# A hybrid attention and mLSTM layer: the FFN in chunks of three and six token blocks, with seven half-size float16 products for the gate and up rows of the six

## The chip, the cores and the metric

The kernel runs on one core of a Trainium2 chip. The core has a matrix engine (PE), whose weight loads are listed as PEld, a vector engine (DVE), an activation engine (ACT), a general engine (POOL), and a queue engine (SP) that issues most DMAs. The metric is device time in microseconds, lower is better; a kernel's time is the median of several runs. Traces come from one profiled execution each.

## The reference

One layer over 9 blocks of 128 tokens (block 0 context, blocks 1 to 8 latent), D = 1024, D_FF = 2816, all in float32. Cut to what matters:

```python
def trunk_layer(x, mods, ...):
    sh1, sc1, g1, sh2, sc2, g2 = mods
    h = rmsnorm(x, norm1_w) * (1 + sc1) + sh1
    aq, ak, av, mq, mk, mv, mo, mg = jnp.split(h @ w_in, SPLIT_POINTS, axis=-1)
    ...
    attn_o = attention(aq, keys, vals)              # 8 query heads, 2 kv heads, 64 wide
    hm, st_f, st_b = mlstm_bidir(...)               # 4 heads, 128 wide, both directions
    ...
    mix = jnp.concatenate([attn_o, hm], axis=-1) @ w_out
    x = x + g1 * mix
    h2 = rmsnorm(x, norm2_w) * (1 + sc2) + sh2
    x = x + g2 * swiglu(h2, w_gu, w_down)

def swiglu(h, w_gu, w_down):
    g, u = jnp.split(h @ w_gu, 2, axis=-1)
    return (jax.nn.silu(g) * u) @ w_down
```

Latent tokens read 128 context keys and all 1024 latent keys. A final norm gives the outputs.

## The kernel before

Float32 accuracy comes from pairs: a value is split into a high part (a cast) and a low part (value minus high), and a product is three matmuls, high with high, high with low, low with high. The input projection has float16 pairs with a common power-of-two scale per weight group; the output projection and the FFN have fp32r pairs without a scale. `load_piece` brings a piece of weights from HBM into `raw` (2 buffers), casts it on ACT into `whi` and subtracts on POOL, or on DVE for each third piece, into `wlo` (5 buffers each). `sub` (L137) is the one line of all such subtractions.

Stages: modulation and normed inputs; query, key, value projections; four mLSTM heads, each head's projection woven with the scan of the head before and with attention of blocks 0 to 2; the mLSTM half of the output projection for all blocks (`prefill`); then the FFN in three chunks of three blocks (`CB` = 3). In a chunk, 22 row tiles f of 128 come in groups of 4 or 5. For each f, `gate_up` runs 24 matmuls for gate and 24 for up over 384 tokens (`products`, L1315 to L1317), applies tanh-form SiLU (L1333 to L1335) and splits the result into `hl`. After a group, `down` multiplies it with `w_down` for both halves n of the output (L1115 to L1117) and adds the gated sum to x1 (`add_gated`, L1104 and L1105).

Beside the first chunk the attention of blocks 3 to 5 is woven in, beside the second that of blocks 6 to 8; behind each comes `attn_out`, the attention half of the output projection, and `norm2` of the next chunk beside the last down group. In attention (`attention`), a head's scores S (L1035, one PSUM tile of three banks) go to DVE for the maximum (L1037), ACT for the exponential (L1038) and the scaled cast (L1041), DVE for the low part (L1042), two DMA transposes, and later 18 value products for a pair of heads (L1059, L1060).

What sets the order: the program is written as generators, `weave` advances a side generator at a rate beside a main one, `hot` raises a priority, and a scheduler orders each engine's instructions by priority and modelled readiness. Every engine then runs its list strictly in order. Buffers are tagged tiles in pools; a new tile waits for the last user of the tile that it replaces.

## Time and profile before

| what | us |
|---|---|
| median of 3 runs (1592.95 to 1603.68) | 1601.16 |
| the profiled execution | 1606.1 |
| its span in the trace | 1604.4 |
| first gate product | 642.1 |
| granted PE clock, mean | 0.973 of full |

The trace is read by stage: the FFN chunks start at 642.1, 963.4 and 1315.3 us. HBM traffic is 183.8 MB read and 13.3 MB written; the largest transfers are 132 gate and up pieces and 72 down pieces, most of 512 KB. Busy time of an engine says little by itself, since matmul records overlap; the distance between starts is a matmul's price in a dense run. Engines other than PE can be idle without cost where PE never waits for them.

### The profile page before, as it was taken

Reading aid. Unit: us, or ns where it says so; the run is one execution under the profiler, and the core shown is the slowest. Engines: PE = TensorE matmul, PEld = TensorE weight load, DVE = VectorE, ACT = ScalarE, POOL = GpSimd, SP = SyncE. Lnnn points to the kernel's source line nnn. Section 1 sums busy time; section 2 is a strip of 40 time slices with the busy share of each in tenths; the row PEclk is TensorE's granted clock in tenths of the full one; section 3 lists DMA queues with packets and bytes.
Section 4 is the critical chain, followed back from the end, with each engine's and each line's share of the span. In section 5 each row is a group of like instructions: output and inputs, shape, how many; then the busy total and the mean of one; then the engine's idle time right before and its main releaser. Section 6 shows DMA issues by size and latency. Waiting matters only on the chain. (4 is left out here: it accounts for less than half of the span.)

```text
span 1604.4 us, 23368 instructions
## 1 busy us (share of the span) xinstructions
PE 1502.1 (94%) x8539; PEld 1252.0 (78%) x8539; DVE 929.7 (58%) x1856; ACT 767.1 (48%) x1409; POOL 658.9 (41%) x526
## 2 busy tenths in 40 slices
PE   6888989899988779999999999999999999999996
PEld 3544557676766567989999989899898989899995
DVE  4778545745747575567443556777764474332445
ACT  4844455856655354535432444555562453333322
POOL 0243532333343443544444444443444445544443
PEclk9899999899999899999999999999999999999998
DMA  9474323442555736867653456887674455544442
GB/s 359 155 198 153 95 53 42 102 77 51 83 138 159 250 106 145 210 173 184 164 153 127 141 151 211 197 179 178 153 177 129 128 151 165 153 128 146 144 128 70
DMA packets 387880, 236.91 MB, mean 148 GB/s; under 512 B 170198, under 2 KB 346790, under 8 KB 387766
## 3 DMA queue, kind: packets, MB, share of 16 engines
q1 hardware_dynamic: 385110, 231.84, 53.7%
q10 hardware_dynamic: 2656, 3.58, 1.0%
q8 instruction: 67, 1.10, 0.3%
q14 instruction: 47, 0.39, 0.1%
HBM read 183.79 MB, written 13.26 MB: 123 GB/s over the span
## 5 line engine op out<-in xcount | busy, mean ns | idle before, releaser
L137 POOL TENSOR_TENSOR wlo<-raw,whi 128x1024 fp32r<-128x1024 f32 (+1 forms) x144 | 349.6, 2431 | 418.3 <-ACT whi L154 392.1
L154 ACT CAST whi<-raw 128x1024 fp32r<-128x1024 f32 (+1 forms) x216 | 221.6, 1026 | 386.3 <-DMA raw<-in_w_gu_dram 136.5
L1316 PE MATMUL mm<-aTl,whi 128*128 128x384 f32 x1056 | 355.1, 336 | 0.0
L1315 PE MATMUL mm<-aTh,whi 128*128 128x384 f32 x1056 | 354.1, 337 | 0.9 <-DVE tn L1334 0.9
L1317 PE MATMUL mm<-aTh,wlo 128*128 128x384 f32 x1056 | 354.7, 336 | 0.0
L1315 PEld LDWEIGHTS mm<-aTh,whi 128*128 128x128 f32 x1056 | 198.2, 188 | 2.2 <-DVE tn L1334 1.5
L1316 PEld LDWEIGHTS mm<-aTl,whi 128*128 128x128 f32 x1056 | 198.4, 188 | 0.8 <-DVE aTl L137 0.2
L1317 PEld LDWEIGHTS mm<-aTh,wlo 128*128 128x128 f32 x1056 | 198.4, 188 | 0.1
L137 DVE TENSOR_TENSOR wlo<-raw,whi 128x1024 fp32r<-128x1024 f32 (+1 forms) x72 | 87.2, 1211 | 150.8 <-ACT whi L154 150.8
L1115 PE MATMUL mm<-whi,hl 128*128 128x512 f32 x372 | 144.9, 393 | 2.7 <-ACT hl L1338 1.4
L1116 PE MATMUL mm<-wlo,hl 128*128 128x512 f32 x372 | 145.7, 393 | 0.0
L1117 PE MATMUL mm<-whi,hl 128*128 128x512 f32 x372 | 142.9, 392 | 1.3 <-POOL hl L137 1.3
L486 PE MATMUL wi<-ipair,hT 128*128 128x384 f16 (+2 forms) x408 | 138.7, 341 | 2.6 <-DVE G L499 1.2
L1042 DVE SCALAR_TENSOR_TENSOR pl<-pr,st,ph 128x1152 f16<-128x1152 f32 (+1 forms) x72 | 107.3, 1491 | 55.6 <-ACT ph L1041 50.7
L487 PE MATMUL wi<-ipair,hT 128*128 128x384 f16 (+2 forms) x408 | 138.2, 339 | 1.3 <-DVE ipair L222 1.3
L488 PE MATMUL wi<-ipair,hT 128*128 128x384 f16 (+2 forms) x408 | 136.5, 340 | 1.7 <-DVE hT L137 1.7
L137 POOL TENSOR_TENSOR hl<-tn,hl 128x384 fp32r<-128x384 f32 x66 | 86.0, 1303 | 98.5 <-ACT hl L1338 98.3
L1038 ACT ACTIVATE pr<-S,st 128x1152 f32<-128x1152 f32 (+1 forms) x72 | 81.5, 1131 | 77.8 <-DVE st L1037 67.5
L1105 DVE TENSOR_TENSOR x<-x,t 128x512 f32<-128x512 f32 x102 | 117.4, 1173 | 0.8
L1334 DVE SCALAR_TENSOR_TENSOR tn<-tn,mm 128x384 f32<-128x384 f32 x66 | 36.4, 551 | 139.7 <-PE mm L1317 97.7
L1037 DVE TENSOR_REDUCE st<-S 128x1 f32<-128x1152 f32 (+1 forms) x72 | 88.8, 1233 | 25.8 <-PE S L1035 25.3
L1035 PE MATMUL S<-kst,qT 128*128 128x384 f32 (+1 forms) x400 | 88.8, 351 | 5.4 <-ACT pr L1038 5.3
(369 smaller groups left out, 2712.9 us busy)
## 6 DMA issues: line engine op xcount, KB each, us to landing
raw<-in_w_gu_dram SPq DMA_DIRECT2D x132, 512.0 KB
raw<-in_w_down_dram SPq DMA_DIRECT2D x60, 512.0 KB
a<-in_w_ada_dram SPq DMA_DIRECT2D x24, 512.0 KB
gl<-g_d SPq DMA_DIRECT2D x36, 256.0 KB
aw<-in_w_ada_dram SPq DMA_DIRECT2D x16, 512.0 KB
iraw<-in_w_in_dram SPq DMA_DIRECT2D x32, 256.0 KB
raw<-in_w_out_dram SPq DMA_DIRECT2D x12, 512.0 KB
x<-in_x_sample_dram SPq DMA_DIRECT2D x11, 512.0 KB
```

Source lines behind the costliest of these rows:

```text
L137: (dve if eng == "dve" else pool).tensor_tensor(out=out, in0=full, in1=hi, op=ALU.subtract)
L154: nc.scalar.copy(hi[:, :n], raw[:, :n])
L486: mm(ps[:, :n], ah, wh[:, k % 2, c0 : c0 + n], start=(k == 0), stop=False)
L487: mm(ps[:, :n], ah, wl[:, k % 2, c0 : c0 + n], start=False, stop=False)
L488: mm(ps[:, :n], al, wh[:, k % 2, c0 : c0 + n], start=False, stop=(k == KD - 1))
L1105: eng.tensor_tensor(out=x1[:, cs], in0=x1[:, cs], in1=t, op=ALU.add)
L1115: mm(ps, ah, wh[:, k % 2, :], start=(k == 0), stop=False)
L1116: mm(ps, ah, wl[:, k % 2, :], start=False, stop=False)
L1117: mm(ps, al, wh[:, k % 2, :], start=False, stop=(k == nk - 1))
L1315: mm(ps, wh[:, k, :], th[:, k, :], start=(k == 0), stop=False)
L1316: mm(ps, wh[:, k, :], tl[:, k, :], start=False, stop=False)
L1317: mm(ps, wl[:, k, :], th[:, k, :], start=False, stop=(k == KD - 1))
```

## The change

The chunks of blocks 3 to 5 and 6 to 8 become one chunk of six, in the order 3, 5, 7, 4, 6, 8 (`SIX`). It needs the attention of all six blocks before it starts, so this moves beside the first chunk (`six_attention`): after each two finished blocks `pair_out` does their attention half of the output projection, the norm, and the transposed, scaled and modulated operand, which goes to HBM (`f_d`), as does x1 (`x1_d`). The weave's rates rise: 0.14 to 0.3 beside the last scan, 0.35 to 0.4 in `prefill`, 50 to 66 steps beside the first chunk; value products of a pair of heads are held back by one pair more.

For the six, `operands` splits each block pair's operand into halves over k (4 tiles of 128 each) and over the two token sets of 384, and forms b11, b21, b22 and the sums t1 to t4, in float16 pairs. `combined(f)` does the same to the weights: gate and up, each in two halves over k, give a11, a12, a22 and s1 to s4. `gate_up_last` then needs seven half products of 4 x 3 matmuls (Winograd's form of Strassen's scheme), with the sums of partial results on DVE, where two times two full products of 24 were needed. Float16 needs a common scale: `norm_scale` bounds the operand, `row_sums` (an absolute sum on ACT of each gate and up piece in the first chunk) bounds the weights, and `power_scale` makes powers of two between the chunks; the scale is undone in the SiLU steps. The weight buffers of f + 1 and f alternate (`w6` in the places b2 and b3, `w1s`). The down products keep fp32r pairs (`down_six`, L1543 to L1545). After the attention the PSUM pool has eight banks.

```diff
-LAST = [(0, 5), (5, 5), (10, 4), (14, 4), (18, 4)]
+LAST = [(0, 2), (2, 4), (6, 4), (10, 4), (14, 4), (18, 4)]
+SIX = [3, 5, 7, 4, 6, 8]
...
+        if bound is not None:
+            bound(raw[:, :n])
...
+                if h % 2 == 0:
+                    if len(late) > 1:
+                        yield
+                        late.pop(0)()
...
+    def row_sums(t):
+
+        def go(raw):
+            jk = ft.tile([P, D], BF16, name=nm("jk"), tag="jk", bufs=1)
+            act(jk, raw, AF.Abs, accum_out=gmx[:, t : t + 1])
+        return go
...
+    def pair_out(p, oT):
...
+        for n in range(2):
+            ws = out_pieces(0, n)
+            for s in range(2):
+                ps = out_block([ws], 0, mix_spare[s], los[s])
+                add_gated(rows[s], ps, g1l[:, n * 512 : (n + 1) * 512], n, pool)
+                yield
...
+            dma(f_d[2 * p + s], f)
...
+    def combined(f):
...
+        for t in raws:
+            act(t, t, AF.Copy, scale=gsc[:, 2:3])
+
+        def split(w, cs, src, eng):
+            nc.scalar.copy(w[:, 0, cs], src)
+            sub(w[:, 1, cs], src, w[:, 0, cs], eng)
+
+        split(w6, slice(0, 1024), g, "pool")
+        dve.tensor_tensor(out=sa[:, lo], in0=u[:, lo], in1=u[:, hi], op=ALU.add)
+        sub(sa[:, hi], sa[:, lo], g[:, lo], "dve")
+        split(w6, slice(1024, 2048), sa, "dve")
+        sub(sb[:, lo], g[:, lo], u[:, lo], "pool")
+        sub(sb[:, hi], g[:, hi], sa[:, hi], "dve")
+        split(w6, slice(2048, 3072), sb, "dve")
+        split(w1, slice(0, 512), u[:, hi], "pool")
...
+    def seven(ps, w, h, first, last):
+        (wh, wl), t = w, h
+        for k in range(4):
+            mm(ps, wh[:, k, :], t[:, 0, k, :], start=(first and k == 0), stop=False, skip_group_check=True)
+            mm(ps, wh[:, k, :], t[:, 1, k, :], start=False, stop=False, skip_group_check=True)
+            mm(ps, wl[:, k, :], t[:, 0, k, :], start=False, stop=(last and k == 3), skip_group_check=True)
...
+            w = a["w"].pop(0)
+            if f + 1 < NF:
+                a["w"].append(combined(f + 1))
...
+            seven(x, w["a11"], hc["b11"], True, False)
+            nc.scalar.copy(c1, x)
+            yield 6
+            seven(y, w["s2"], hc["t2"], True, False)
+            dve.tensor_tensor(out=u2, in0=y, in1=c1, op=ALU.add)
+            yield 6
+            seven(z, w["s1"], hc["t1"], True, False)
+            nc.scalar.copy(p5, z)
+            yield 6
+            seven(x, w["a12"], hc["b21"], False, True)
+            yield 6
+            seven(y, w["s3"], hc["t3"], False, False)
+            dve.tensor_tensor(out=u3, in0=y, in1=c1, op=ALU.add)
+            yield 6
+            seven(z, w["s4"], hc["b22"], False, True)
+            yield 6
+            seven(y, w["a22"], hc["t4"], False, True)
...
-    weave(scan, beside((ada, 0.5), (first, 0.35), (att, 0.14)), 37, 37)
+    weave(scan, beside((ada, 0.5), (first, 0.35), (att, 0.3)), 37, 37)
...
+    weave(main, att, 18 * sum(nf for _, nf in GROUPS[:NG]) - 24, 66)
+    emit(att)
+    es_at.close()
+    psum["mm"] = ctx.enter_context(tc.tile_pool(name="p8", bufs=8, space=PSUM, reuse_waits="tile"))
```

On PE, in the gate and up stretch of the last chunk before, the full gate product ends and the up product of the same f begins (`whi`, `wlo` are weight pieces, `aTh`, `aTl` the operand's parts):

```order
L1315 MATMUL mm_2602_13480<-aTh_2543_13137,whi_2607_13512 128x384
L1316 MATMUL mm_2602_13480<-aTl_2544_13138,whi_2607_13512 128x384
L1317 MATMUL mm_2602_13480<-aTh_2543_13137,wlo_2608_13513 128x384
L1315 MATMUL mm_2621_13584<-aTh_2543_13137,whi_2624_13587 128x384
L1316 MATMUL mm_2621_13584<-aTl_2544_13138,whi_2624_13587 128x384
L1317 MATMUL mm_2621_13584<-aTh_2543_13137,wlo_2625_13588 128x384
```

On PE, in the chunk of six after, the first half product of a tile ends (a11 with b11, into x) and the second begins (s2 with t2, into y):

```order
L1466 LDWEIGHTS w6_2375_11840
L1466 MATMUL mm_2394_11992<-hc_2177_10745,w6_2375_11840 128x384
L1467 LDWEIGHTS w6_2375_11840
L1467 MATMUL mm_2394_11992<-hc_2177_10745,w6_2375_11840 128x384
L1468 LDWEIGHTS w6_2375_11840
L1468 MATMUL mm_2394_11992<-hc_2177_10745,w6_2375_11840 128x384
L1466 LDWEIGHTS w6_2375_11840
L1466 MATMUL mm_2395_11993<-hc_2177_10745,w6_2375_11840 128x384
L1467 LDWEIGHTS w6_2375_11840
L1467 MATMUL mm_2395_11993<-hc_2177_10745,w6_2375_11840 128x384
L1468 LDWEIGHTS w6_2375_11840
L1468 MATMUL mm_2395_11993<-hc_2177_10745,w6_2375_11840 128x384
```

The products keep their width of 384 and are float16 now; weight loads are instructions of their own, and a new weight part begins after 12 products instead of 24.

On DVE, between two tiles of the last chunk before:

```order
L137 TENSOR_TENSOR wlo_14616<-raw_14614,whi_14615 128x1024
L1334 SCALAR_TENSOR_TENSOR tn_14506<-tn_14506,mm_14445 128x384
L1335 TENSOR_TENSOR tn_14506<-tn_14506,mm_14444 128x384
L1334 SCALAR_TENSOR_TENSOR tn_14575<-tn_14575,mm_14514 128x384
L1335 TENSOR_TENSOR tn_14575<-tn_14575,mm_14513 128x384
```

On DVE, around one tile of the six after (c, p and u are sums of partial results, `tn` the SiLU product, `w6` the weight parts of a later tile):

```order
L1485 TENSOR_TENSOR u2_2415_12132<-mm_2411_12128,c1_2413_12130 128x384
L1508 SCALAR_TENSOR_TENSOR tn_2401_12090<-tn_2401_12090,gsc_104,c1_2397_11995 128x384
L1493 TENSOR_TENSOR u3_2416_12133<-mm_2411_12128,c1_2413_12130 128x384
L1500 TENSOR_TENSOR p5_2414_12131<-u3_2416_12133,p5_2414_12131 128x384
L1499 TENSOR_TENSOR u2_2415_12132<-mm_2412_12129,u2_2415_12132 128x384
L141 TENSOR_TENSOR w6_2422_12244<-sa_2423_12245,w6_2422_12244 128x1024
L141 TENSOR_TENSOR w6_2422_12244<-sb_2424_12246,w6_2422_12244 128x1024
L1506 SCALAR_TENSOR_TENSOR tn_2419_12233<-tn_2419_12233,p5_2414_12131 128x384
L1501 TENSOR_TENSOR c1_2413_12130<-mm_2411_12128,c1_2413_12130 128x384
```

Two operations a tile and a third of a weight piece have become nine and two weight parts, most of them with both inputs in SBUF.

On ACT, beside the first chunk, two weight casts before with two heads' exponentials:

```order
L1038 ACTIVATE pr_1519_7543,st_1522_7546<-S_1523_7547,st_1522_7546 128x1152
L154 CAST whi_1490_7386<-raw_1489_7385 128x1024
L1041 ACTIVATE ph_1520_7544<-pr_1519_7543,st_1522_7546 128x1152
L1062 ACTIVATE ol_1525_7593<-po_1524_7574,vsc_94 64x256
L154 CAST whi_1496_7440<-raw_1495_7439 128x1024
L1038 ACTIVATE pr_1539_7634,st_1542_7637<-S_1543_7638,st_1542_7637 128x1152
```

and a like piece after (L1110 are the row sums, L1289 and L1297 the norm in `pair_out`):

```order
L158 CAST whi_1684_8283<-raw_1683_8282 128x1024
L1110 ACTIVATE jk_1686_8288,gmx_6483<-raw_1683_8282 128x1024
L158 CAST whi_1699_8370<-raw_1698_8369 128x1024
L1033 CAST qT_1663_8197<-mm_1664_8198 64x4x128
L1062 ACTIVATE pr_1657_8176,st_1660_8179<-S_1661_8180,st_1660_8179 128x1152
L1110 ACTIVATE jk_1701_8375,gmx_6483<-raw_1698_8369 128x1024
L1297 ACTIVATE xr_1665_8207<-mm_1667_8210,sc6_105 128x128
L1289 ACTIVATE y_1692_8349<-xr_1578_7804,ry_1650_8127 128x512
```

Each gate or up piece now has a second reading on ACT, between the steps of the heads and of the output projection.

More of the change, by code (lines that the diff above doesn't have):

```diff
@@ L139, in hybrid_step, with load_piece @@
     lo_count = [0]
-    def load_piece(srcs, shape, dve_every=3, raw=None, own=None):
+    def load_piece(srcs, shape, dve_every=3, raw=None, own=None, bound=None):
         a, b = shape
@@ L979, in hybrid_step @@
     emit(ada)
+    emit(norm_scale())
     emit(kwork)
@@ L1069, in attention @@
                     late.append(values)
-        late.pop()()
-        yield
+        for v in late:
+            v()
+            yield
     def new_oT():
@@ new lines, in hybrid_step @@
+    w1s = [w1s[:, i] for i in range(2)]
+    one1 = np2.tile([1, P], F32, name="oneb")
+    dve.memset(one1, 1.0)
+    f0, nf = GROUPS[-1]
+    ops = chain(*[operands(np2, i, hc) for i in range(3)])
+    weave(gate_up(cur, f0, nf), ops, 12 * nf, 8)
+    emit(ops)
+    gmax = np2.tile([P, 1], F32, name="gmax")
+    dve.tensor_reduce(out=gmax, in_=gmx[:, 0 : 2 * NF], axis=AX.X, op=ALU.max)
+    scale = power_scale(np2, one1, gmax, gsc[:, 2:4])
+    last = {"x1": x1}
+    for i, _ in enumerate(chain(down(0, cur, f0, nf, 0), down(0, cur, f0, nf, 1))):
+        if i < 2:
+            with hot(1000):
+                next(scale, None)
+            emit(scale) if i == 1 else None
+        elif i == 2:
+            dve.tensor_tensor(out=gsc[:, 4:5], in0=gsc[:, 1:2], in1=gsc[:, 3:4], op=ALU.mult)
+            dve.tensor_scalar(out=gsc[:, 5:6], in0=gsc[:, 4:5], scalar1=0.5, scalar2=None, op0=ALU.mult)
+            es_n.close()
+            wx = ctx.enter_context(tc.tile_pool(name="wx", bufs=1, side="right", reuse_waits="tile"))
+            last["w"] = [combined(0)]
@@ L1498, with groups_last @@
+    def groups_last():
+        for f0, nf in LAST[:-1]:
+            yield from gate_up_last(last, hc, f0, nf)
+            yield from down_six(last, f0, nf, 0)
+            yield from down_six(last, f0, nf, 1)
+    main = groups_last()
+    for _ in range(4):
+        next(main)
+    weave(main, finish(0, cur), 48, 3)
+    emit(main)
+    emit(gate_up_last(last, hc, *LAST[-1]))
+    down_last(last, *LAST[-1])
 TC_OPTS = dict(schedule_with_timeline_sim=True)
```

396 lines of the change are left out of this document (242 added, 154 removed).

## The prediction

> **What bounds the kernel now.** I read the page first, then busy time by stage, the groups by form, and the timeline where two kinds of product run densely.
>
> ```profile
> span 1604.4 us, 23368 instructions
> PE 1502.1 (94%) x8539; PEld 1252.0 (78%) x8539; DVE 929.7 (58%) x1856; ACT 767.1 (48%) x1409; POOL 658.9 (41%) x526
> ...
> 535.00:642.00 107.00, 86.62 (x408) 67.14 (x407) 63.14 (x140) 46.76 (x72) 43.36 (x31) 0.89 0.61 167
> 642.00:963.40 321.40, 321.25 (x1751) 295.07 (x1751) 175.71 (x243) 138.09 (x181) 146.30 (x73) 1.00 0.60 162
> 963.40:1315.30 351.90, 346.95 (x1924) 317.29 (x1922) 228.71 (x330) 176.47 (x234) 149.48 (x71) 1.00 0.65 167
> 1315.30:1604.40 289.10, 274.35 (x1455) 257.18 (x1453) 123.27 (x195) 94.73 (x131) 134.88 (x69) 0.98 0.45 136
> ```
>
> The columns of a stage are its length, then busy time of PE, PEld, DVE, ACT and POOL, granted clock, DMA share and GB/s. The last three rows are the FFN chunks of three blocks: PE is busy 321.25 of 321.40, 346.95 of 351.90, and in the last chunk all but the 14.75 us tail, at clock 1.00. TensorE is the bound from 642 us to the end. So the change is worth the PE time that it takes out there, less the stalls that it puts in. Only ahead of 642 us has PE room: 20.4 us idle between 535 and 642.
>
> ```profile
> 1399.76 0.33 PE L1315 MATMUL mm<-aTh,whi 128*128 128x384 f32 x1
> ...
> 1409.47 0.33 PE L1317 MATMUL mm<-aTh,wlo 128*128 128x384 f32 x1
> ...
> 254.39 0.33 PE L486 MATMUL wi<-ipair,hT 128*128 128x384 f16 x1
> ...
> 258.12 0.33 PE L488 MATMUL wi<-ipair,hT 128*128 128x384 f16 x1
> ...
> 1421.60 0.39 PE L1115 MATMUL mm<-whi,hl 128*128 128x512 f32 x1
> 1421.83 0.40 PE L1116 MATMUL mm<-wlo,hl 128*128 128x512 f32 x1
> 1422.06 0.40 PE L1117 MATMUL mm<-whi,hl 128*128 128x512 f32 x1
> ```
>
> Durations of matmuls overlap, so the price is the distance of starts. The first pair of rows has 56 distances: 9.71/56 = 0.1734 us for a 128x384 fp32r product. The second has 23: 3.73/23 = 0.1622 us for the same shape in float16. A down product (128x512) takes 0.23 us.
>
> **The products of the six.** Before, a row tile f costs 48 products a chunk, 96 for six blocks: 2112 over 22 tiles, 2112 x 0.1734 = 366.2 us. After, seven half products of 4 x 3 matmuls are 84 per f, 1848 in all: 1848 x 0.1622 = 299.7 us. That is 66.5 us less on the engine that bounds: 264 products fewer are worth 45.8, the float16 rate 20.7.
>
> **Attention and its output for six blocks beside the first chunk.** The order puts 32 of the 72 heads (192 score products) behind the first gate product of the first chunk, where before 12 stood in the first chunk and 24 in the second. Each of these two chunks also carried the output projection and norm of three blocks. Against the last chunk, which has neither, PE is busy 321.25 - 274.35 = 46.9 us more with 12 heads and 346.95 - 274.35 = 72.6 us more with 24. So 12 heads are 25.7 us, 2.14 a head, and three blocks' output 21.2 us. The new first stage is 274.35, less 42 down products that the order lets run among the six's (9.7), plus 32 x 2.14 = 68.5, plus 42.4: 375.6 us of PE work. Four heads move ahead of 642 us, 8.6 us. They are free if they fill the 20.4 us idle there and cost 8.6 if not; the idle is only partly next to them, so I take 4.
>
> Is the cover there? By the same differences a block of 12 heads is 38.4 us of ACT and 53 us of DVE.
>
> ```profile
> 963.40:1180.00 216.60, 212.98 (x1215) 196.01 (x1214) 153.97 (x214) 119.29 (x157) 90.21 (x41) 1.00 0.74 185
> ...
> L1278 ACT ACTIVATE jk<-x 128x1024 bf16<-128x1024 f32 x15 | 15.8, 1053 | 16.1 <-POOL x L1105 9.3 <-DVE x L1105 6.8
> L154 ACT CAST whi<-raw 128x1024 fp32r<-128x1024 f32 x204 | 214.2, 1050 | 360.0 <-DMA raw<-in_w_gu_dram 136.5 <-PE mm L1117 61.1 <-PE mm L1316 59.4
> ```
>
> ACT gets 94.7 + 32 x 3.2 + 5 of output, plus the 44 new row sums. Their nearest row is the square sum L1278, 1.05 us, with about 0.2 for reading the accumulator: 55 us. Splitting the operands of the six adds 21 casts of 128x512 at half of L154, 11 us. That is 268 of some 386 us, 69%. DVE gets 123.3 + 32 x 4.4 + 12 = 276 us, 72%. DMA: the last chunk moves 0.45 x 289 = 130 us, twelve heads 36 and an output 27 (same differences), so 130 + 96 + 54 and about 25 for the x1 and operand rows through HBM: 305 us, 79%. The attention part of the second chunk, first row of the fence, had 71% DVE, 55% ACT and 74% DMA, and PE was busy 98%. ACT is what is fuller now. Idle PE there: at least 0 (the first chunk had 0.15), 6.6 by the second chunk's 4.95 us on 24 heads, and at the far end 88 (PE 81% busy, the row 535 to 642). I take 10, near the second chunk, and 385.6 us for the stage.
>
> **The six's chunk.** PE: 299.7 + 834 down products x 0.23 = 191.8, 491.5 us. The tail of 14.75 stays: block by block it is the same chain, and its order on DVE has not changed. What must hide is the making of seven weight parts per f within 84 x 0.1622 = 13.63 us.
>
> ```profile
> L137 POOL TENSOR_TENSOR hl<-tn,hl 128x384 fp32r<-128x384 f32 x66 | 86.0, 1303 | 98.5 <-ACT hl L1338 98.3
> L137 DVE TENSOR_TENSOR wlo<-raw,whi 128x1024 fp32r<-128x1024 f32 x66 | 83.0, 1258 | 125.5 <-ACT whi L154 125.4
> L1335 DVE TENSOR_TENSOR tn<-tn,mm 128x384 f32<-128x384 f32 x66 | 36.5, 552 | 1.7
> L1333 ACT ACTIVATE tn<-mm 128x384 f32<-128x384 f32 x66 | 32.0, 485 | 10.9 <-PE mm L1317 10.7
> L137 POOL TENSOR_TENSOR ipair<-iraw,ipair 128x1024 f16<-128x1024 f32 x10 | 22.6, 2264 | 18.8 <-ACT ipair L225 18.8
> L224 ACT ACTIVATE iraw<-iraw,isc 128x1024 f32<-128x1024 f32 x10 | 10.9, 1145 | 0.0
> L225 ACT CAST ipair<-iraw 128x1024 f16<-128x1024 f32 x10 | 10.5, 1054 | 2.3 <-PE wi L488 2.3
> ...
> 1584.88 1.29 POOL L1400 TENSOR_TENSOR x<-x,fw 128x512 f32<-128x512 f32 x1 [7.15 <-ACT jk L1397]
> 1584.91 1.81 DVE L1105 TENSOR_TENSOR x<-x,t 128x512 f32<-128x512 f32 x1
> ...
> 1587.64 0.68 DVE L1105 TENSOR_TENSOR x<-x,t 128x512 f32<-128x512 f32 x1
> ```
>
> Per f, ACT: two scalings 2.3, three and a half casts 3.7, eight evacuations and casts of 384 at 0.49, 3.9: 9.9 us. DVE: three sums of 128x512 at 0.68, two lower parts at 1.26, nine operations of 384 at 0.55: 9.5 us. POOL: lower parts of 1024 and 512 (2.26 and 1.29), one difference 1.29, two hl of 1.30: 7.4 us. Alone, each fits into 13.63. But the last three rows show DVE and POOL in each other's way: the add that takes 0.68 us took 1.81 when it started 0.03 us behind a POOL multiply of 1.29. Its operands all lie in SBUF. Of DVE's work per f such operations are three sums, two lower parts and five of the nine: 2.04 + 2.52 + 2.76 = 7.3 us. If they exclude POOL's 7.4, the two need 14.7 us in 13.63: 1.1 us a tile, 24 us over 22 tiles. At the other end it is 0, because each down stretch (144 x 0.23 = 33 us a group) lets them catch up and the weights run one tile ahead. I take the middle, 12 us.
>
> The Trainium skill, page "SBUF — State Buffer", section "Who interferes with whom", says that a DVE instruction with two SBUF inputs and a GpSimd instruction that reads SBUF exclude each other for the whole instruction. By that rule the upper end, 24 us, is the sum and the forecast would be 12 us later; the row of 1.81 us agrees.
>
> Also new, and hidden: the common scale between the chunks (a transpose, a small product and some DVE steps), covered by the 90 down products of the last group, 20.7 us. If that cover is missed, the first tile's parts are late once, by 5 to 10 us; this lies inside the idle taken.
>
> **Sum.** 642.0 + 4 ahead, 385.6 first stage, 491.5 + 12 + 14.75 for the six: 1550 against the span of 1604.4, 54 us less. The profiled execution took 1606.1, 0.3% over the median 1601.2, so I subtract from the median: 1547.
>
> **The rivals.**
> Exclusion sets the pace: DVE and POOL cost the full 24 us and, being in-order queues, lose as much again in hand-overs, 1 us a tile: 12 becomes 47, time 1582. For it speak the 14.7 against 13.63; against it the order, where the casts of a tile's weights stand one whole tile ahead.
> Attention stalls the first stage: with ACT and DMA near 70 and 80%, a score product waits for the exponential of the head before and PE, in order, with it. At 89% busy, between the 98 and 81% seen, idle is 45 for 10: 1582.
> The half products don't get the float16 rate and take 0.1734 us, so that part of the change does nothing: 20.7 more, 1568. Against it stand 23 distances in a row with the same operands' types and shape.
> Slower: the weight parts come late in every tile. Buffer b2 or b3 comes free with the last product of the tile before; three casts (3.2), a POOL part (2.26), two DVE parts (2.5) and a wait for the port (2.3) are 10.3 us behind it. If PE has to stand for part of this in each tile, the gain without the 12, 66 us, is gone at 3.0 us a tile; at 4.5 us the time is 1547 - 12 + 99 = 1634. Against it: the chain has 13.63 us of products to hide under, and parts used last may come last.
>
> **How the numbers follow.** Forecast 0.62, its own range 1525 to 1570; exclusion 0.15; attention 0.10; no float16 rate 0.06; late weights 0.07. A measurement of this kernel tells about 1% from no change, so faster is under 1585 and slower over 1617. Faster: 0.62 + 0.06 and the larger parts of the two rivals at 1582 (0.09 + 0.06), 0.83. Same: what is left of these, 0.10. Slower: 0.07. The range 1520 to 1590: the low end is every idle term at 0 and the moved heads free (1547 - 26 = 1521). Above it lie the late weights (0.07) and the upper ends of the two rivals (0.07); below it some 0.04.
>
> **What would show it.** Starts of the half products 0.162 us apart and 1848 of them; the first stage near 386 us with PE over 95% busy; the six's chunk near 518 us with PE idle under 30 us before the tail. Waits of the half products for w6's lower parts show the exclusion or late weights; waits of score products for the exponential show the attention rival. A first stage over 430 us, or a tile over 17 us in the gate stretches, would make the prediction wrong.

## The result and the profile after

| | median of the runs | lowest to highest | profiled execution | its span |
|---|---|---|---|---|
| before | 1599.04 us (4 runs) | 1592.95 to 1603.68 | 1606.1 us | 1604.4 us |
| after | 1618.63 us (4 runs) | 1613.77 to 1624.27 | 1618.65 us | 1616.8 us |

The changed kernel is 1.3% slower: 1.0126 times the time before, 95% interval 1.0077 to 1.0175. The forecast was 1547 us, its range 1520 to 1590, and a slower kernel had 0.07. Cut at the same three events as the prediction's sum, the profiled execution shows where the 67 us are:

| | forecast | measured | difference |
|---|---|---|---|
| start to first gate product | 646 | 637.9 | -8.1 |
| first stage, to the first half product | 385.6 | 427.4 | +41.8 |
| six's chunk and tail | 518.3 | 551.5 | +33.2 |
| span | 1550 | 1616.8 | +66.9 |

The last two stretches of the changed kernel, in the view by windows (bounds, length, busy time and instructions of PE, PEld, DVE, ACT, POOL, then the granted clock, the DMA share, GB/s):

```profile
core 0: us, PE busy (x) PEld busy (x) DVE busy (x) ACT busy (x) POOL busy (x), PEclk, DMA share, GB/s
637.90:1065.30 427.40, 388.79 (x2120) 341.90 (x2118) 283.22 (x405) 274.51 (x407) 203.57 (x104) 0.97 0.74 190
1065.30:1616.80 551.50, 509.60 (x2683) 339.03 (x2682) 407.71 (x536) 239.04 (x358) 264.04 (x158) 0.97 0.25 77
```

ACT at 274.5 us, DVE at 283.2 and DMA at 0.74 are within 8 us or 0.05 of the prediction's loads for this stage. PE is not: 388.8 us busy for 375.6, and 38.6 idle for 10. In the second row PE stands 41.9 us, tail included.

**What the arithmetic gave.** The first product of a tile of the six, the first of the next tile, and the first of the next group, from the timeline of PE (start, length, operation):

```profile
1260.66 0.33 PE L1466 MATMUL mm<-hc,w 128*128 128x384 f16 x1
1274.43 0.33 PE L1466 MATMUL mm<-hc,w 128*128 128x384 f16 x1
...
1328.41 0.34 PE L1466 MATMUL mm<-hc,w 128*128 128x384 f16 x1
```

The first two are 13.77 us apart: 84 half products 0.1639 us apart, for 0.1622 forecast. Most tiles that a tile follows take 13.65, which is 0.1625 a product. So 1848 of them take 300 to 303 us for the 366 of the products that they replace, and the saving was nearly all there. The third is 53.98 us behind the second. A tile (13.77) and the 144 down products of a group (33.1 at 0.23) make 46.9: 7 us are lost at this group's end, inside a stretch that the prediction took for slack.

**What is lost at a group's end.** The same place on DVE, POOL and PE, from the timelines, each engine apart:

```profile
1294.98 1.63 DVE L1506 SCALAR_TENSOR_TENSOR tn<-tn,p 128x384 f32<-128x384 f32 x1 [1.06 <-ACT tn L1505]
1296.54 2.32 DVE L141 TENSOR_TENSOR w<-sa,w 128x1024 f16<-128x1024 f32 x1
1298.78 2.50 DVE L1508 SCALAR_TENSOR_TENSOR tn<-tn,gsc,p 128x384 f32<-128x384 f32 x1
1301.20 0.55 DVE L1501 TENSOR_TENSOR c<-mm,c 128x384 f32<-128x384 f32 x1
1302.80 1.85 DVE L141 TENSOR_TENSOR w<-sb,w 128x1024 f16<-128x1024 f32 x1
1304.58 0.60 DVE L1508 SCALAR_TENSOR_TENSOR tn<-tn,gsc,c 128x384 f32<-128x384 f32 x1
...
1296.16 1.61 POOL L141 TENSOR_TENSOR sb<-raw,raw 128x512 f32<-128x512 f32 x1
1297.73 3.13 POOL L141 TENSOR_TENSOR w<-raw,w 128x1024 f16<-128x1024 f32 x1
1300.82 1.48 POOL L141 TENSOR_TENSOR w1s<-raw,w1s 128x512 f16<-128x512 f32 x1
1302.27 1.31 POOL L141 TENSOR_TENSOR hl<-tn,hl 128x384 fp32r<-128x384 f32 x1
...
1301.88 0.50 PE L1543 MATMUL mm<-whi,hl 128*128 128x512 f32 x1 [0.32 <-ACT hl L1515]
1303.63 0.50 PE L1545 MATMUL mm<-whi,hl 128*128 128x512 f32 x1 [0.56 <-POOL hl L141]
1305.78 0.79 PE L1543 MATMUL mm<-whi,hl 128*128 128x512 f32 x1 [1.66 <-ACT hl L1515]
```

A row's length here holds its wait for the other engine. `w<-sa,w` of DVE begins 0.4 us behind POOL's `sb<-raw,raw` and takes 2.32 us; POOL's `w<-raw,w`, begun at 1297.73, takes 3.13; the product `tn<-tn,gsc,p` of DVE, begun at 1298.78 inside it, 2.50. The row at 1301.20, with one operand in PSUM, takes 0.55 beside POOL's 1.48. That `tn` is the activation of the group's last tile. Its casts come late, and the last three rows show PE waiting for them three times, 2.5 us; the clock, below, takes about 3 us more. The groups by line of the chunk (busy, mean ns of one, idle before them) show that this is the rule there:

```profile
L141 DVE TENSOR_TENSOR w<-sa,w 128x1024 f16<-128x1024 f32 x20 | 43.7, 2187 | 17.1 <-ACT w L1446 17.1
L1506 DVE SCALAR_TENSOR_TENSOR tn<-tn,p 128x384 f32<-128x384 f32 x19 | 27.8, 1465 | 2.0 <-ACT tn L1505 2.0
L141 POOL TENSOR_TENSOR w<-raw,w 128x1024 f16<-128x1024 f32 x19 | 43.2, 2274 | 59.2 <-ACT w L1446 57.1 <-issue 2.1
L1501 DVE TENSOR_TENSOR c<-mm,c 128x384 f32<-128x384 f32 x19 | 10.4, 545 | 0.0
```

In the trace of before, DVE's `wlo<-raw,whi`, a like subtraction of 128x1024, had a mean of 1258 ns: 44 of the 66 had no GpSimd instruction beside them. Here `w<-sa,w` has 2187: 2 of the 20 had none beside them and took 1.21 and 1.22 us, the other 18 took 1.85 to 2.38. `c<-mm,c`, with an operand in PSUM, keeps its 545, also where a GpSimd instruction runs all through it. The Trainium skill, "SBUF — State Buffer", section "Who interferes with whom", states this exclusion for DVE instructions with two SBUF inputs and none for those with at most one outside the two-port modes; the 2.50 and the 0.55 agree with both halves.

**What is lost at the first group's end.** The first group of the six has two tiles and 72 down products. From the start of its second tile to the start of the third are 48.6 us (1091.88 to 1140.43), where a tile (13.65) and 72 products at 0.23 make 30.2. The longest of PE's waits there, 13 us in all, with what stands ahead of it on ACT:

```profile
1106.24 1.04 ACT L158 CAST whi<-raw 128x1024 fp32r<-128x1024 f32 x1 [5.30 <-DMA raw<-in_w_down_dram]
1107.19 0.47 ACT L1488 COPY p<-mm 128x384 f32<-128x384 f32 x1
1107.71 0.48 PE L1466 MATMUL mm<-hc_b,w 128*128 128x384 f16 x1 [7.87 <-ACT p L1488]
```

PE's next product adds to a PSUM bank that ACT has to copy out first, and ACT, in order, stands 5.3 us at the cast of a down weight piece that has not landed. Two stretches of 6.8 us at half clock fall into this time as well.

**What is lost in the first stage.** The longest wait of PE, the one ahead of the first half product, and what DVE and POOL did in the first:

```profile
978.01 0.40 PE L1142 MATMUL mm<-whi,hl 128*128 128x512 f32 x1
988.98 1.11 PE L120 MATMUL mm<-ident,y 128*128 128x128 f32 x4 [10.57 <-ACT y L1289]
...
1063.86 1.65 PE L1140 MATMUL mm<-whi,hl 128*128 128x512 f32 x3 [4.76 <-ACT whi L158]
...
977.72 0.17 DVE L131 TENSOR_SCALAR rv<-s 128x2 f32<-128x2 f32 x1 [2.05 <-ACT jk L1351]
977.92 2.25 DVE L132 TENSOR_SCALAR rh<-rv 128x2 int32<-128x2 int32 x1
980.20 2.26 DVE L133 TENSOR_SCALAR ry<-rh 128x2 int32<-128x2 int32 x1
982.50 0.16 DVE L135 TENSOR_TENSOR rt<-ry 128x2 f32<-128x2 f32 x1
...
977.78 4.66 POOL L141 TENSOR_TENSOR wlo<-raw,whi 128x1024 fp32r<-128x1024 f32 x2
```

PE stands 10.57 us, in order, at the transposes of the last pair's norm (`y`), with down products of this group and the gate products of the last one behind them in its list. They need twelve operations of DVE on 128x2 numbers, some 0.16 us each. Four of them take longer beside GpSimd: `rh` and `ry` 2.25 and 2.26 us, and end as the two low parts `wlo` of GpSimd from 977.78 on end (4.66 us for both); two later ones take 1.11 and 1.10. The second wait, 4.76 us, is for the last down weights' cast: the cover for the transition is missed, the case that the prediction priced at 5 to 10 us. Waits of score products for the exponential, the sign named for the rival on attention, come four times and make 5.5 us.

**The clock.** Two stretches each, one ahead of a change of the granted clock and one behind it, in the view by windows:

```profile
977.50:980.90 3.40, 0.91 (x4) 0.38 (x3) 3.11 (x3) 0.19 (x2) 3.40 (x3) 1.00 1.05 398
980.90:994.50 13.60, 5.52 (x15) 4.55 (x16) 12.26 (x22) 7.41 (x14) 7.51 (x5) 0.50 0.56 185
1301.80:1305.20 3.40, 1.70 (x5) 0.86 (x5) 3.31 (x4) 2.57 (x4) 2.19 (x3) 1.00 0.89 257
1305.20:1312.00 6.80, 6.22 (x15) 4.86 (x16) 6.66 (x7) 2.63 (x3) 4.03 (x3) 0.50 0.09 26
```

Before the change, the rows from 642 to 1315 us had a granted clock of 1.00. Now a wait costs twice: 13.6 us at half speed begin in the 11 us wait and reach 5.5 us into the products behind it. In the first stage such stretches add to 26 us.

### The profile page after: what moved, and what is told of

Read it like the earlier page. It is cut to its first block, busy times and chain, and to the rows that moved or that the text cites. A ratio compares the mean times of both kernels' runs of the same rounds, so it can differ in the third digit from the quotient of the medians.

```text
span 1616.8 us, 23138 instructions
## 1 busy us (share of the span) xinstructions
PE 1461.6 (90%) x8281; PEld 1070.9 (66%) x8281; DVE 1111.1 (69%) x2063; ACT 885.2 (55%) x1649; POOL 699.7 (43%) x576
## 3 DMA queue, kind: packets, MB, share of 16 engines
q8 instruction: 65, 1.06, 0.3%
## 5 line engine op out<-in xcount | busy, mean ns | idle before, releaser
L141 POOL TENSOR_TENSOR wlo<-raw,whi 128x1024 fp32r<-128x1024 f32 x71 | 173.1, 2440 | 229.2 <-ACT whi L158 205.8
L158 ACT CAST whi<-raw 128x1024 fp32r<-128x1024 f32 (+1 forms) x106 | 108.7, 1027 | 98.6 <-DMA raw<-in_w_down_dram 48.1
L1388 PE MATMUL mm<-aTh,whi 128*128 128x384 f32 x352 | 120.2, 341 | 1.2 <-DVE qT L141 1.2
L1390 PE MATMUL mm<-aTh,wlo 128*128 128x384 f32 x352 | 120.2, 342 | 0.0
L1389 PE MATMUL mm<-aTl,whi 128*128 128x384 f32 x352 | 120.1, 341 | 0.0
L1466 PE MATMUL mm<-hc,w 128*128 128x384 f16 x352 | 115.7, 329 | 1.0 <-ACT c L1482 1.0
L1467 PE MATMUL mm<-hc,w 128*128 128x384 f16 x352 | 115.6, 329 | 0.0
L1468 PE MATMUL mm<-hc,w 128*128 128x384 f16 x352 | 115.4, 328 | 0.0
L1061 DVE TENSOR_REDUCE st<-S 128x1 f32<-128x1152 f32 (+1 forms) x72 | 88.7, 1232 | 17.5 <-PE S L1052 17.0
L1065 ACT ACTIVATE ph<-pr,st 128x1152 f16<-128x1152 f32 (+1 forms) x72 | 83.8, 1164 | 26.2 <-issue 9.0
L1543 PE MATMUL mm<-whi,hl 128*128 128x512 f32 x216 | 87.2, 414 | 11.5 <-ACT hl L1515 6.0
L1544 PE MATMUL mm<-wlo,hl 128*128 128x512 f32 x216 | 87.9, 407 | 0.0
L1545 PE MATMUL mm<-whi,hl 128*128 128x512 f32 x216 | 84.0, 406 | 1.9 <-POOL hl L141 1.9
L1130 POOL TENSOR_TENSOR xr<-xr,t 128x512 f32<-128x512 f32 x34 | 52.7, 1550 | 64.9 <-DVE t L1129 54.6
```

The costliest lines, as they stand in the source:

```text
L141: (dve if eng == "dve" else pool).tensor_tensor(out=out, in0=full, in1=hi, op=ALU.subtract)
L158: nc.scalar.copy(hi[:, :n], raw[:, :n])
L1388: mm(ps, wh[:, k, :], th[:, k, :], start=(k == 0), stop=False)
L1389: mm(ps, wh[:, k, :], tl[:, k, :], start=False, stop=False)
L1390: mm(ps, wl[:, k, :], th[:, k, :], start=False, stop=(k == KD - 1))
L1466: mm(ps, wh[:, k, :], t[:, 0, k, :], start=(first and k == 0), stop=False, skip_group_check=True)
```

## The experiments

The stage below is from the first gate product to the first half product, 427.4 us in the changed kernel; the chunk is all behind it, 551.5 us. Single executions of the kernel before lie up to 11 us apart, and all experiments but e13 and e16 were executed once, so the lengths of the stages in the traces carry the argument. The first stage, which e2 and e3 leave as it is, had 427.1 and 429.2 us in them.

**e1_no_sums.** `row_sums` is not called, and the bound is a constant:

```diff
-                    wh, wl = load_piece([(full_view, src)], (KD, P), bound=row_sums(f + NF * (off > 0)))
+                    wh, wl = load_piece([(full_view, src)], (KD, P))
...
-    dve.tensor_reduce(out=gmax, in_=gmx[:, 0 : 2 * NF], axis=AX.X, op=ALU.max)
+    dve.memset(gmax, 28.169256)
```

> Leaves out the 44 row sums of the weights on ScalarE; the weights' bound is a constant instead. Theory A (in the first stage ScalarE, loaded by the sums, is late for the exponentials and weight casts that TensorE waits for): the stretch from the first gate product to the first half product goes from 427 us to 405 or less. Theory B (TensorE there waits at places that the attention's order makes, the last pair's norm above all, whatever ScalarE's load): it stays between 418 and 430. The six blocks' chunk stays within 5 us of 551 under both.

```profile
634.40:1045.80 411.40, 384.05 (x2121) 338.00 (x2119) 281.43 (x405) 233.39 (x325) 197.47 (x104) 0.98 0.77 198
```

The stage is 411.4 us, between the two theories: 16 us of the 42 go with the sums, and the wait of 11 us at the last pair's transposes is still there. The chunk is 550.3. The time is 1598.2 us, the kernel before beside it 1600.6.

**e2_high_only.** In `combined` and `gate_up_last` the low parts that POOL makes are left out:

```diff
+            if eng != "pool":
                 sub(w[:, 1, cs], src, w[:, 0, cs], eng)
...
+        out["a11"] = (w[:, 0, 0], w[:, 0, 0])
+        out["a12"] = (w[:, 0, 1], w[:, 0, 1])
...
-                sub(hl[:, 1], tn, hl[:, 0].bitcast(F32), "pool")
...
-        return hl[:, 0, cs], hl[:, 1, cs]
+        return hl[:, 0, cs], hl[:, 0, cs]
```

> Leaves out, in the six blocks' chunk, the low parts that GpSimd makes of the gate and up weights (a11, a12, a22) and of the activations; TensorE multiplies by the high part in their place, so its work is the same. Theory C (VectorE and GpSimd hold each other up there, and TensorE waits for the activations at the end of a group): the chunk goes from 551 us to 530 or less, the mean of the wide w<-sa,w subtraction on VectorE from 2.19 us to under 1.6. Theory D (the rate is set by TensorE's own products and a clock at half speed): it stays within 6 us of 551.

```profile
1061.60:1585.10 523.50, 500.93 (x2683) 336.81 (x2682) 341.17 (x534) 240.47 (x358) 130.28 (x74) 0.98 0.27 81
```

The chunk is 523.5 us, 28 shorter, and `w<-sa,w` takes 1377 ns. Theory C holds, theory D falls: PE's work is the same and 28 us are gone. It does not yet tell the exclusion from the mere amount of work; the next does better.

**e3_one_engine.** GpSimd has nothing left to do for the six ahead of the tail:

```diff
-        split(w6, slice(0, 1024), g, "pool")
+        split(w6, slice(0, 1024), g, "dve")
...
-        sub(sb[:, lo], g[:, lo], u[:, lo], "pool")
+        sub(sb[:, lo], g[:, lo], u[:, lo], "dve")
-        split(w1, slice(0, 512), u[:, hi], "pool")
+        split(w1, slice(0, 512), u[:, hi], "dve")
...
-                sub(hl[:, 1], tn, hl[:, 0].bitcast(F32), "pool")
+                sub(hl[:, 1], tn, hl[:, 0].bitcast(F32), "dve")
...
-            pieces.append(load_piece([(full_view, rows)], (m, 512)))
+            pieces.append(load_piece([(full_view, rows)], (m, 512), 1))
...
-                add_gated(a["x1"][i], ps, g(i), n, pool if i % 2 else dve)
+                add_gated(a["x1"][i], ps, g(i), n)
```

> Same values, with all that GpSimd does in the six blocks' chunk moved to VectorE. Theory C (it is the two engines' mutual exclusion that costs, not the amount of work): VectorE's busy time in the chunk falls or stays near 400 us although it takes over 264 us of GpSimd's, and the chunk goes from 551 to 535 or less. Theory E (the elementwise work is simply too much or its chain too long): VectorE becomes the bound and the chunk is 560 or more. First stage unchanged within 5 us of 427 under both.

Both stretches, and three groups by line of the chunk:

```profile
634.00:1063.20 429.20, 389.18 (x2120) 343.36 (x2118) 283.96 (x413) 275.33 (x407) 192.65 (x99) 0.97 0.74 190
1063.20:1587.00 523.80, 501.62 (x2683) 337.96 (x2682) 401.40 (x683) 239.24 (x357) 11.95 (x8) 0.98 0.26 80
...
L141 DVE TENSOR_TENSOR w<-sa,w 128x1024 f16<-128x1024 f32 x21 | 25.6, 1218 | 0.0
L1506 DVE SCALAR_TENSOR_TENSOR tn<-tn,p 128x384 f32<-128x384 f32 x22 | 12.1, 552 | 1.5 <-ACT tn L1505 1.5
L141 DVE TENSOR_TENSOR w<-raw,w 128x1024 f16<-128x1024 f32 x20 | 24.4, 1222 | 5.4 <-ACT w L1446 5.4
```

DVE took over some 250 us of POOL's time and is busy 401.4 us where it was 407.7. What POOL did in 2274 ns, DVE does in 1222, and its own operations are back at 1218 and 552. The chunk is 523.8 us. From the start of a group's last tile to the next group's first product are 47.2 to 47.5 us in the four groups of four; they were 50.2 to 54.0. The time is 1588.8 us, against 1600.6. So 27.7 us of the chunk came from the work of both engines side by side. DVE took 147 instructions more without being busy longer, and that is the exclusion gone; a part of the 27.7 may be GpSimd's own pace, since its shortest subtraction of 128x1024 took 2.13 us, and e3 does not separate the two.

The forecast's 518.3 us already held 12 for the exclusion. Without any it is 506.3, and the measured 551.5 are 45.2 above that: 27.7 that e3 takes away, and 17.5 that stay. Of these, the first group's end has most: 44.9 us there in e3, where 30.2 would do.

**e4_ahead.** More attention ahead of the stage:

```diff
-        due += 0.4
+        due += 0.7
...
-    weave(main, att, 18 * sum(nf for _, nf in GROUPS[:NG]) - 24, 66)
+    weave(main, att, 18 * sum(nf for _, nf in GROUPS[:NG]) - 24, 68)
```

> More of the six blocks' attention before the first stage (33 steps of 89 in place of 24) and an earlier end of the rest beside it. Theory B (the attention's order stalls TensorE in the first stage): the first gate product comes up to 25 us later, the first stage shrinks by more than that, at least 35 us, from 427 to 392 or less, and the 11 us wait before the last pair's transposes is gone; net 10 to 25 us gained. Theory A (ScalarE's load): what is moved is only paid earlier, the sum of both changes by less than 6 us.

The first gate product came at 661.2 us, 23 later, and the stage took 411.8, 16 less; the time was 1625.4. Both theories miss: the stage shrank by less than half of the 35 us, and the sum of both grew by 7.7. PE's idle time in the stage stayed 39.2 us, with waits of 7.4 and 3.2 us for the last probabilities' low parts and their transposes, and of 7.0 at the norm. With less attention beside the chunk PE stood as long, and nearly half of it at the attention's end.

**e5_first_too and e7_max_on_vector**, both on top of e3_one_engine, put work on DVE in the stage. In e5 all of POOL's work there (weights, activations, operands, adds) goes to DVE by the same kind of edit as in e3. In e7 the bound comes from magnitudes:

```diff
-            act(jk, raw, AF.Abs, accum_out=gmx[:, t : t + 1])
+            dve.tensor_reduce(out=gmx[:, t : t + 1], in_=raw, axis=AX.X, op=ALU.max, apply_absolute_value=True)
...
+    dve.tensor_scalar(out=gmax, in0=gmax, scalar1=4.0, scalar2=None, op0=ALU.mult)
```

> Same values; e3_one_engine, and GpSimd's work on the first stage's weights, activations and operands goes to VectorE as well. If mutual exclusion of the two engines also holds the first stage back (theory C there), it falls from 429 us to 415 or less. If VectorE's load is the nearer limit in that stage (it would do about 350 us of work in it), the stage grows to 435 or more. Chunk of the six within 5 us of 524 either way.

> Same values within float16 pairs' rounding; e3_one_engine, with the weights' bound from four times their largest magnitude, which VectorE finds (44 instructions) in place of ScalarE's row sums. Theory A (it is ScalarE's load that the sums hurt by): the stage falls from 429 to about 413, as without sums, if VectorE has the room. Rival: about 50 us more of VectorE work does the same harm, the stage stays at 424 or more.

The stage of e5, then of e7:

```profile
634.30:1068.80 434.50, 393.83 (x2120) 348.15 (x2118) 320.76 (x507) 277.87 (x407) 2.47 (x2) 0.95 0.73 188
```

```profile
638.90:1091.70 452.80, 402.96 (x2140) 353.92 (x2139) 327.42 (x456) 236.85 (x327) 192.99 (x100) 0.95 0.71 182
```

434.5 and 452.8 us, for 429.2 in e3: the repair of the chunk does not carry over, and it is the rival's side both times (e5 half a microsecond under its bound of 435). DVE is 321 and 327 us busy in place of 284. In e7 PE stands 9.9 us longer than in e3; in e5 it stands as long (40.7 us for 40.0) and is slower, with 47 us at half clock for 28. In e5 no GpSimd runs beside DVE, and each of the twelve small operations takes 0.15 or 0.16 us; yet the wait at the norm is 14.5 us, because DVE's other work, in rows of 0.68 to 1.23 us, stands between them. So what makes the norm late is not the exclusion alone. Times 1590.4 and 1616.9 us, beside 1597.8.

**e6_norm_behind**, on top of e3: one tile of the last group stands ahead of the last pair's norm, and the weave's rate falls from 66 steps to 61.

```diff
-    weave(main, att, 18 * sum(nf for _, nf in GROUPS[:NG]) - 24, 66)
+    weave(main, att, 18 * sum(nf for _, nf in GROUPS[:NG]) - 24, 61)
+    f0, nf = GROUPS[-1]
+    emit(gate_up(cur, f0, 1))
+    ahead = cur["act"]
     emit(att)
...
+    cur["act"] = ahead + cur["act"]
```

> Same values; e3_one_engine, with the gate and up products of one tile of the last group put ahead of the last pair's transposes on TensorE. Theory B (TensorE stands 11 us at those transposes while these products are ready): the wait is under 4 us and the first stage falls from 429 to 420 or less, by 8 us and some more where the clock's half-speed window behind the wait goes too. Rival: the chain behind the last pair (transposes, operands, first half product) sets the end of the stage, the wait comes back at its end, and the stage stays within 4 us of 429.

```profile
635.20:1056.20 421.00, 392.67 (x2121) 342.28 (x2119) 274.78 (x411) 275.10 (x407) 188.77 (x99) 0.97 0.76 194
```

The stage is 421.0 us, 8 less than e3's and 1 over the bound; the wait is 4.7 us and not under 4. The chunk is 518.7. The time is 1576.8 us, 21 under the kernel before beside it (1597.8), where e3 and e5 were 12 and 7 under theirs.

**The sums again: e8_all, e9_vector_no_sums, e10_sums_twice.** e8 is e6 with the sums left out as in e1, e9 is e3 with them left out, and e10 is the changed kernel with the line that takes a sum written twice.

> e3_one_engine and e6_norm_behind together, and without the row sums (their result is a constant, as in e1_no_sums). If the three causes are independent, the gains add: 1616.8 less 30 (vector engine alone), less 16 to 20 (sums), less 8 to 12 (norm), a span of 1554 to 1563 us, near the forecast of 1550 for the change itself. If they share the same idle time, the span stays above 1570.

> e3_one_engine without the row sums (a constant in their place). If the sums' load on ScalarE costs the first stage 16 us whatever else changes, the stage goes from 429 to about 413. If that gain came from the order that the scheduler happened to make of e1_no_sums, it lies anywhere from 415 to 430 here.

> The changed kernel with every row sum taken twice, 44 more of 1.25 us on ScalarE, 55 us. If the load of the sums is what stalls the first stage (theory A), it grows from 427 by 15 us or more, most of it as TensorE waits for exponentials, casts and the activations' high parts. If ScalarE's load there is harmless at 300 of 427 us, the stage stays below 435.

The stages of e9 and e10:

```profile
635.30:1044.70 409.40, 382.40 (x2120) 337.09 (x2118) 281.46 (x413) 234.33 (x325) 189.15 (x99) 0.98 0.76 199
```

```profile
635.30:1080.70 445.40, 398.56 (x2141) 350.71 (x2139) 288.61 (x408) 319.23 (x491) 202.14 (x105) 0.96 0.71 185
```

e9 takes 19.8 us off e3's stage and e10 puts 18.0 on, 8 of it idle, with one wait of 9.1 us for a transpose by DMA and not most of it at the places expected. With e1 these are three pairs in which the sums cost the stage 16 to 20 us. The sums are rows of 1.06 and 0.19 us that overlap a little: ACT's busy time changes by 41 to 45 us. e8 has 419.6 us, 1.4 less than e6, and a span of 1578.2, on the side of shared idle time (above 1570). With the norm behind a tile, the sums cost nothing.

The same runs read the other way: moving the norm gains 8 us with the sums (e3 to e6) and loses 10 without them (e9 to e8, where PE waits 10.6 us at the norm all the same). e9, which leaves the norm where it was and takes a constant for the sums, is the fastest version: 1568.9 us, beside 1596.7 for the kernel before.

**e11_buffers and e12_buffers_hot**, on top of e6:

```diff
-            raw = (wx if f % 2 else wp).tile([P, 1024], F32, name=nm("raw"), tag="raw", bufs=2)
+            raw = (wp if f % 2 else wx).tile([P, 1024], F32, name=nm("raw"), tag="raw", bufs=2)
```

and in e12 also `with hot(1000):` around the pairs' `stats(rows)`.

> Same values; e6_norm_behind, with the raw buffers of the first tile of the six taken from the new pool instead of the one that the last down weights of the first stage use. If those weights come late because the two raw buffers are held by the tile of the six that waits for the scale (theory: 5 us wait just ahead of the first half product), that wait falls under 1.5 us and the chunk's start comes 4 to 5 us earlier. If it is the transfer itself, the wait stays.

> Same values; e11_buffers, with the pairs' square sums and reciprocal roots scheduled ahead of VectorE's and ScalarE's other work. If the last pair's norm is late because its small operations queue behind the operands' and adds' on VectorE, the remaining wait of the transposes (5 us in e6_norm_behind) falls under 2 us and the first stage by 3 to 6 us against e11_buffers. Rival: other work of VectorE that TensorE also waits for is then later by as much, and the stage stays within 3 us.

The wait ahead of the first half product fell to 0.7 us in e11, as the theory has it, and the first half product came 3.4 us earlier; but the chunk grew by 8.6 us, to 527.3: the first group's end takes 48.9 us for e6's 39.6, with waits for partial results and activations. The time was 1581.8 us; the gain was paid back twice over. e12's stage is 5.7 us shorter than e11's, but its wait at the transposes is still 4.6, so not by the way expected. Its chunk is 528.7 us, its time 1577.5.

**Do the norm and the sums share one cause? e13_hot, e14_hot_no_sums, e16_last_pair, e17_last_pair_no_sums.** e13 is e6 with the `hot` of e12 and the old buffers, e16 is e6 with the last pair's adds on DVE and these, the square sums and the roots put ahead; e14 and e17 are the same two without the sums.

```diff
+                with hot(1000 if p == 2 else 0):
+                    add_gated(rows[s], ps, g1l[:, n * 512 : (n + 1) * 512], n, dve if p == 2 else pool)
...
+        with hot(1000 if p == 2 else 0):
+            rs = stats(rows)
```

> Same values; e6_norm_behind with the pairs' square sums and reciprocal roots scheduled ahead of other work, the buffers as in the changed kernel. From the stage of e12_buffers_hot and the chunk of e6_norm_behind: 635 + 414 + 519, a span of 1568 (1562 to 1575), faster than the kernel before by 1.5 to 2.4%. If the two gains exclude each other (another order of the chunk), 1575 or more.

> e13_hot without the row sums (a constant in their place). If the sums' load and the late norm are separate causes, the first stage loses another 12 us or more against e13_hot, to 402 or less, near the 386 forecast. If they meet in the same wait (ScalarE and VectorE are late for the last pair's norm because of the sums), the stage stays within 6 us of e13_hot's, as e8_all stayed within 2 us of e6_norm_behind's.

> Same values; e6_norm_behind with the last pair's adds on VectorE and its adds, square sums and roots scheduled ahead of other work. If the chain of the last pair (add, square sum, root, scaling, transposes) is what TensorE stands at, because each of its steps queues behind operands' work or a GpSimd low part, the wait of 5 us there falls under 2 and the stage from 421 to 415 or less, the span to 1569. If VectorE's queue there is as long whoever owns it, the stage stays at 418 to 424.

> e16_last_pair without the row sums (a constant in their place). One cause: within 6 us of e16_last_pair's stage, as e14 stayed with e13. Two causes: 12 us or more below it.

e13's stage and chunk, then e14's stage and its wait at the norm:

```profile
635.70:1055.70 420.00, 389.74 (x2121) 340.59 (x2120) 281.72 (x413) 276.22 (x407) 191.63 (x99) 0.96 0.76 194
1055.70:1578.00 522.30, 501.06 (x2683) 337.21 (x2682) 401.45 (x683) 239.34 (x357) 12.03 (x8) 0.98 0.26 81
```

```profile
633.70:1053.70 420.00, 391.24 (x2120) 341.93 (x2119) 293.84 (x411) 233.49 (x325) 187.40 (x99) 0.96 0.77 194
...
993.36 1.97 PE L120 MATMUL mm<-ident,y 128*128 128x128 f32 x8 [10.71 <-ACT y L1290]
...
983.41 2.83 DVE L1130 TENSOR_TENSOR x<-x,t 128x512 f32<-128x512 f32 x1
986.16 2.30 DVE L131 TENSOR_SCALAR rv<-s 128x2 f32<-128x2 f32 x1
988.50 0.17 DVE L132 TENSOR_SCALAR rh<-rv 128x2 int32<-128x2 int32 x1
...
982.89 5.55 POOL L141 TENSOR_TENSOR wlo<-raw,whi 128x1024 fp32r<-128x1024 f32 x2
```

The stages are 420.0, 420.0, 419.9 and 419.4 us. The priorities changed nothing (e13's span is 1578.0 for the 1568 expected; e16's wait at the norm fell to 3.2 us, the stage stayed), and neither did the sums: without them the wait at the last pair is back, 10.7 us in e14 and 12.8 in e17, in e14 with one root step of 128x2 at 2.30 us and an add of 128x512 at 2.83 beside POOL's two low parts from 982.89 on. By the terms set beforehand that is one cause, not two. What is shown is less: with the sums, moving the norm helps, and without them it hurts; taking the sums away helps only where the norm is not moved. Each such edit also gives the scheduler another order of the work, and no run here holds that order fixed, so how much of the 8 to 20 us is the order is open. Timed, e13 is 0.9884 times the kernel before (0.9862 to 0.9905; 1581.2 us), e16 0.9889 (0.9859 to 0.9918; 1582.1 us): both beat the kernel before, by 1.1 to 1.2%, and the changed one.

## Why the prediction was wrong

**The products of the six** held: 0.1625 to 0.1639 us apart for 0.1622, the work 300 to 303 us for 299.7.

**The four heads ahead of the first gate product** show no cost; it came 4 us earlier than before, where 4 later were taken.

**The step that failed in the six's chunk is "I take the middle, 12 us".** It was 27.7 by e3, over the upper end of 24, and the reason given for the lower end was the wrong one: that each down stretch "lets them catch up". The tiles themselves kept PE's pace, 13.65 to 13.77 us. The down stretch is where it was paid, some 18 of the 27.7 us at the ends of the four groups of four, because its first products need the activations of the tile just done, and their chain over DVE and ACT runs while both engines are still at the weights of the next tiles. The sum of busy times asked whether the work fits, and not how late one operation comes out. The rival "exclusion sets the pace" put 47 us there, as a pace per tile, which the tiles do not show. Late weights in every tile, the slower rival, did not happen: one tile between others, the last but one, was late, with 18.1 us from its start to the next one's; in e3 it takes 13.65.

**The step that failed in the first stage is "I take 10, near the second chunk".** The loads that it was argued from came out right, and the idle time was 38.6 us. Two things are new against the chunks of before. One is the sums on ACT, which the prediction counted into the load and gave no price in PE's time: 16 to 20 us by e1 and e9, where the norm stays in its place. The other is a last norm that must be done before a chunk of six can begin, on PE's list ahead of other products: a wait of 10.6 us, of which e6 got 8 us of stage back, though without the sums the same edit lost 10. These prices do not add up to the 42 us, and the share of the scheduler's order is open. A part is PE work that was priced at full clock: e9, without the sums and with the wait at the norm still in it, has 382.4 us busy and 27.0 idle for 375.6 and 10, with 20 us of it at half clock.

**The step that failed at the transition is "this lies inside the idle taken".** The missed cover, priced at 5 to 10 us, came with 4.8 us ahead of the first half product. Behind it the first group's end lost some 18 us, 14.7 of them also in e3, and the sum has no term for it. e11 suggests that the two belong together: it takes the wait away, and the first group's end grows by more. What sets this loss, the late down weights, ACT's order or the output of the first chunk that stands beside it, no run separates.

**The way the chances were made** failed as well. The two rivals at 1582 were taken as alternatives, 0.15 and 0.10. Losses of both sizes came together: 1547 + 33 + 42 - 8 is 1614, and the range ended at 1590. By mechanism they came only in part: the exclusion at the groups' ends and not in every tile, and 38.6 us idle for the attention rival's 45, of which the score products' waits are 5.5. That both have one root, fuller DVE, ACT and POOL, is likely and not shown; they had to be added where they were.

## What to carry to other kernels

When VectorE and GpSimd both work on pairs of operands in SBUF, price an operation by the other engine's longest instruction that it may find, and price it at the place where the chain ends on which TensorE waits, not by the sum of busy times; where the work is short of filling VectorE alone, all of it on VectorE can take less time (e3), and in a stage where the chains that TensorE waits for run through VectorE it did not (e5, e7). A stage that is followed by one that needs all of its results has an end, and so has the new stage a beginning; both need a term of their own in the sum. Ready products ahead of those that wait for the last chain can help there (e6), but the next order of the work can take it back (e8). Losses that can come side by side are added, not chosen between.

## What was not expected of the hardware

An operation on 128x2 numbers with one operand in SBUF took 2.25 us beside a GpSimd subtraction of 128x1024, and 0.16 in e5 with no GpSimd beside it: so an operation this small is held up, and with one operand too. The Trainium skill, "SBUF — State Buffer", section "Who interferes with whom", allows this: it counts `tensor_scalar` among the operations that can enter a two-port mode and then exclude GpSimd. And the clock went to half behind a stretch of 3.4 us in which PE had been busy 1.70 (1301.80, above), in waits none of which was over 1.7 us. The Trainium skill, "TensorE: Matmul & The Clock Gate", section "What's actually happening", gives an idle window of about 3.4 us as the condition; here a window about half busy could be enough. Counted in steps of 3.41 us from the clock's changes, another window of this trace with 1.70 us busy, from 946.80 on, was followed by full clock, and each with under 1.5 us busy by half. And every half-speed stretch of the changed kernel's first stage and chunk, eight of them with the tail's, lasted a multiple of 3.4 us, or ended with the program.
